# Layer 1 of a two-layer recurrent trunk: one compact tile for an item's beta and kappa, and what the scores and transposes then take

## The chip, the cores and the metric

The kernel runs on one core of a Trainium2 chip. The metric is the device time of one execution in microseconds (us), as a median over runs. The profile is of one execution, and its own time stands beside its span below. Engine names are those of the profile: PE is TensorE's matmul stream and PEld its weight loads, DVE is VectorE, ACT is ScalarE, POOL is GpSimd, SP is the queue that issues most DMAs.

## The reference

Layer 0 is a gated DeltaNet mixer, layer 1 an RWKV-7 mixer, then a final RMSNorm; 1024 prompt tokens behind 16 meta tokens and 8 samples of 8 tokens go through both, 1104 tokens in all. The change lies in layer 1. Cut to what matters, it computes for 16 heads of 64 channels:

```python
kk = l2norm((k * k_k).reshape(B, T, H, N))
k = k * (1.0 + (a - 1.0) * k_a)
decay = jnp.exp(-jnp.exp(w))
b_h = kk * a_h
def step(S, inp):
    S = (S * d_t[:, :, None, :]
         + jnp.einsum('bhvk,bhk->bhv', S, -kk_t)[..., None] * b_t[:, :, None, :]
         + v_t[..., None] * k_t[:, :, None, :])
    return S, jnp.einsum('bhvk,bhk->bhv', S, r_t)
```

and, behind the scan, a norm per head, a bonus term, a gate and the projection `y @ w_o`.

## The kernel before, in words

Everything is float32; large projections are split into a high and a low part of a faster format (fp32r), so a product is three matmuls (`whi`/`wlo` are the parts of a weight, `d`, `dz`, `zz` their outputs). Two stages matter here. Up to about 1885 us of the span run layer 0, the projections of layer 1 and the inverses of the chunks' triangular matrices. From there to the end runs layer 1's recurrence, in `layer1`, and with it the gate projections of the later token segments (`zz`), the output projection (`d<-yh`, `d<-yl`) and the final norm (`dfin`).

The recurrence works on 24 items: 3 token segments (384, 384, 336 tokens) times 8 pairs of heads. An item is a tile of 128 rows, 64 channels of each of the two heads, by 384 tokens, which are 6 chunks of 64. For each item `rwkv_front` prepares:

- `AR`, per chunk 64 columns of decayed alpha and 64 of decayed receptance;
- beta and kappa (`BK`), 64 columns each per chunk: the key times an inverse decay, by DVE, and the rate times the normalised key, by POOL. There are two persistent tiles `BK[0]` and `BK[1]` of 128 rows each. They are zeroed once (L1715), and an item writes rows 0 to 63 of the one and rows 64 to 127 of the other, so that a matmul over 128 rows of `BK[h]` sees head h alone;
- scores `G` = BK' AR, a 128x128 block for each chunk and head: 12 matmuls over 128 rows, three to a PSUM tile, masked into SBUF by DVE;
- `BT`, the transposed BK: 12 transposes, one per chunk and head, of a head's 64 rows;
- `UV`, whose first 64 rows are the transposed v: 6 transposes, one per chunk, into two PSUM tiles.

All these PSUM tiles share the name `f`, of which there are two buffers; so the third tile waits until the first has been copied out. `rwkv_step` then does one chunk of one item (outputs `rA`; `rX`, `UV`, `rS` on the way), and three items are in their steps at any time. `rwkv_finish` ends an item (`zyT`, `yh`, `yl`). A float32 matmul is two instructions on PE (two passes), a transpose one.

The Python loop over `tau` names the work, but the order on each engine is set when the program is built, by a scheduler that goes through the instructions with times of its own. So an edit of the front also moves other instructions. Each engine then runs its own list in order and waits on semaphores. In the listings the numbers behind names tell copies of a tile apart; the scores of the item numbered 10 (the third pair of the second segment) are `G_26195` before and `G_26080` after.

In the profile a matmul's form is written as rows*columns of the stationary operand, then the moving one: `128*64 128x128` has 128 rows, 64 columns, and 128 moving columns. I call rows*columns its tile shape. `64*128` stands for a head's 64 rows.

Of the kernel before, what the change touches and what calls it, by code (L numbers as in the profile page):

```python
# [11 lines left out]
ALU = mybir.AluOpType  # L12
# [23 lines left out]
class Builder:  # L36
# [8 lines left out]
    def t(self, pool, shape, tag, bufs=1, dt=F32):  # L45
        self.uid += 1
        return pool.tile(shape, dt, name=f"{tag}_{self.uid}", tag=tag, bufs=bufs)
# [1275 lines left out]
    def rwkv_front(self, p, s):  # L1323
        nc, t, ap, col = self.nc, self.t, self.ap, self.pcol
        P = Ctx()
        P.n = 8 * s + p
        NB = self.NB
        pc = lambda n: col[n][:, p:p + 1]
        P.TT = t(ap, [128, 6, 64], "rTT", 3)
        nc.sync.dma_start(P.TT.rearrange("p c k -> p (c k)"), self.ttd[P.n])  # L1330
        ld = self.rwkv_load(P.n, ap, "f", ("cs", "k", "a", "r", "v"))
        kk, Dp, iD = self.rwkv_keys(p, ld, ap, "f")
        DC = P.DC = t(ap, [128, 14], "DC", NB + 2)
        nc.gpsimd.tensor_copy(DC[:, 0:6].unsqueeze(2), Dp[:, 1:385].rearrange("p (c k) -> p c k", k=64)[:, :, 63:64])
        if s == 0:
            nc.gpsimd.tensor_copy(DC[:, 6:14].unsqueeze(2), Dp[:, 1:65].rearrange("p (c k) -> p c k", k=8)[:, :, 7:8])
        AR = P.AR = t(ap, [128, 6, 2, 64], "AR", NB)
        c6 = lambda x: x.rearrange("p (c k) -> p c k", k=64)
        self.alpha(AR[:, :, 0, :], kk, Dp, s, nc.gpsimd)
        nc.vector.tensor_tensor(AR[:, :, 1, :], c6(ld["r"]), c6(Dp[:, 1:385]), op=ALU.mult)  # L1340
        k2 = t(ap, [128, 384], "k2", 1)
        self.act(k2, ld["a"], AF.Identity, scale=pc("rwkv_k_a"), bias=self.omka[:, p:p + 1])
        nc.vector.tensor_tensor(k2, k2, ld["k"], op=ALU.mult)
        nc.gpsimd.tensor_tensor(kk, kk, ld["a"], op=ALU.mult)

        for h in (0, 1):
            q = slice(64 * h, 64 * h + 64)
            nc.vector.tensor_tensor(self.BK[h][q, :, 0, :], c6(k2)[q], c6(iD)[q], op=ALU.mult)
            nc.gpsimd.tensor_tensor(self.BK[h][q, :, 1, :], c6(kk)[q], c6(iD)[q], op=ALU.mult)
        flat = lambda x: x.rearrange("p x k -> p (x k)")  # L1350

        pr = t(ap, [128, 384], "pr", 1)
        nc.vector.scalar_tensor_tensor(pr, ld["r"], pc("rwkv_r_k"), k2, op0=ALU.mult, op1=ALU.mult)
        bp = self.ps("f", 2, "bonus")
        ph, pl = t(ap, [128, 384], "prh", 1, F32R), t(ap, [128, 384], "prl", 1, F32R)
        self.split(pr, ph, pl, "act", "pool")
        self.mm(bp[:, 0:384], self.bones, ph, start=True, stop=False)
        self.mm(bp[:, 0:384], self.bones, pl, start=False, stop=True)
        bv = P.bv = t(ap, [128, 384], "rbv", NB + 1)
        nc.vector.tensor_tensor(bv, ld["v"], bp[:, 0:384], op=ALU.mult)  # L1360

        G = P.G = t(ap, [128, 6, 2, 128], "G", NB)
        for c in (0, 3):
            for h in (0, 1):
                gp = self.ps("f", 2, "G")
                for u in range(3):
                    self.mm(gp[:, 128 * u:128 * u + 128], flat(self.BK[h][:, c + u]), flat(AR[:, c + u]))
                g3 = gp[:, 0:384].rearrange("p (q k) -> p q k", k=128)
                f = 0
                if s == 0 and c == 0:  # L1370
                    nc.vector.tensor_tensor(G[:, 0, h, :], g3[:, 0, :], self.gms, op=ALU.mult)
                    f = 1
                nc.vector.tensor_tensor(G[:, c + f:c + 3, h, :], g3[:, f:3], self.gm.unsqueeze(1).broadcast_to([128, 3 - f, 128]),
                                        op=ALU.mult)

        BT = P.BT = t(ap, [128, 6, 128], "BT", NB)
        UV = P.UV = self.UVs[P.n % len(self.UVs)]
        for h in (0, 1):
            q = slice(64 * h, 64 * h + 64)
            tp = self.ps("f", 2, "BT")  # L1380
            for c in range(6):
                self.transpose(tp[:, 64 * c:64 * c + 64], flat(self.BK[h][q, c]))
            nc.scalar.copy(BT[:, :, q], tp[:, 0:384].rearrange("p (c k) -> p c k", k=64))
        for c in (0, 3):
            vp = self.ps("f", 2, "VT")
            for u in range(3):
                self.transpose(vp[0:64, 128 * u:128 * u + 128], ld["v"][:, 64 * (c + u):64 * (c + u) + 64])
            nc.scalar.copy(UV[0:64, c:c + 3].rearrange("p c h k -> p (c h k)"), vp[0:64, 0:384])
        return P

    def rwkv_step(self, p, s, P, ci):
# [289 lines left out]
    def layer1(self, ctx, right, stay, xa, xb, x):  # L1681

        nc, tc = self.nc, self.tc
# [6 lines left out]
        for n, (m, k) in enumerate(todo):  # L1690
            if k == 0:
                x = self.mix(m, xb)
# [14 lines left out]
        t, ap = self.t, self.ap  # L1707
# [2 lines left out]
        self.X = [t(ap, [128, 2, 64], f"rX{q}") for q in range(4)]  # L1710
        NB = self.NB = 4
        self.UVs = [t(ap, [128, 6, 2, 64], f"UV{q}") for q in range(NB)]
        self.BK = [t(ap, [128, 6, 2, 64], f"BK{q}") for q in (0, 1)]
        for x in self.BK + self.X + self.UVs + self.S:
            nc.vector.memset(x, 0.0)  # L1715
        P, yo, todo = {}, {}, []
        gates = (None for s in (1, 2) for _ in self.rwkv_gates(xa, s, self.fin))
# [3 lines left out]
        for tau in range(-LAG * AHEAD, LAG * 24 + 6):  # L1721
            n = tau // LAG + AHEAD
            if tau % LAG == 0 and 0 <= n < 24:
                s, p = divmod(n, 8)
# [10 lines left out]
            for n in range(max(0, (tau - 5 + LAG - 1) // LAG), min(24, tau // LAG + 1)):  # L1735
                s, p = divmod(n, 8)
# [53 lines left out]
```

## Time and profile before

| what | value |
|---|---|
| median of 3 runs | 2517.23 us (2510.52 to 2519.47) |
| the profiled execution: its own time | 2503.36 us |
| its span | 2501.6 us |
| granted TensorE clock over the span | 0.968 |
| PE busy | 2305.2 us (92%), 18593 instructions |
| DVE, ACT, POOL busy | 1698.5 (68%), 1423.3 (57%), 1148.4 us (46%) |

The profile page gives for each engine how long at least one of its instructions was under way. On PE instructions overlap: one that lasts 275 ns may have its successor start 112 ns later. So for the cost of a matmul what counts is the distance from its start to the start of the next. The timeline view lists start and length of each group of like instructions; the start of the row below less the start of a row is what the group took of PE.

### The profile page before, as it was taken

To read this page: it belongs to the slowest core of one execution; us is meant where nothing else is said; L and a number is where in the kernel's file an instruction comes from. 1 tells how busy PE (TensorE), PEld (TensorE's weight loads), DVE (VectorE), ACT (ScalarE), POOL (GpSimd) and SP (SyncE) were. 2 spreads that over 40 slices of the span, in tenths; PEclk is the share of its full clock that TensorE was granted. 3 is DMA by queue.
4 is the path that set the end of the run, shared out by engine and by line. 5 is a ranking of instruction groups with operands and counts; after the bars stand their busy time and mean duration, and the time that the engine had idled before them with its cause. 6 is when DMAs were issued, how large, how long until landed. Compare 5 with 4: busy or idle time off the path is not lost. (4 is left out here: it accounts for less than half of the span.)

```text
span 2501.6 us, 52567 instructions
## 1 busy us (share of the span) xinstructions
PE 2305.2 (92%) x18593; PEld 2065.5 (83%) x18593; DVE 1698.5 (68%) x4268; ACT 1423.3 (57%) x3913; POOL 1148.4 (46%) x1404
## 2 busy tenths in 40 slices
PE   6998999999898989999989999988879999999996
PEld 5887988888797889789989998877768777877875
DVE  7779686876849585863357535697875678667563
ACT  5456555564646565565344557464444567678663
POOL 4554444444444354432214425453347565656653
PEclk9999999999999999999999999999988999999997
DMA  3323333333232333353251445767565444343331
GB/s 107 100 72 98 83 106 83 95 85 85 79 91 77 87 89 85 92 147 118 89 147 60 117 167 180 170 184 202 145 181 170 126 133 121 94 140 88 110 97 50
DMA packets 471939, 284.65 MB, mean 114 GB/s; under 512 B 187482, under 2 KB 457051, under 8 KB 471675
## 3 DMA queue, kind: packets, MB, share of 16 engines
q1 hardware_dynamic: 471674, 281.29, 40.0%
q8 instruction: 147, 2.41, 0.4%
q14 instruction: 118, 0.96, 0.1%
HBM read 200.00 MB, written 81.17 MB: 112 GB/s over the span
## 5 line engine op out<-in xcount | busy, mean ns | idle before, releaser
L86 POOL TENSOR_TENSOR wlo<-wraw,whi 128x512 fp32r<-128x512 f32 x260 | 347.8, 1340 | 350.9 <-ACT whi L82 311.9
L82 ACT CAST whi<-wraw 128x512 fp32r<-128x512 f32 x260 | 160.1, 617 | 168.7 <-PE dq L76 43.6
L76 PE MATMUL d<-xc,whi 128*128 128x384 f32 (+3 forms) x846 | 238.2, 339 | 0.3 <-ACT ev L1152 0.3
L450 DVE TENSOR_TENSOR invtmp<-invA,invT 72x31 f32<-72x31 f32 (+31 forms) x403 | 184.7, 458 | 20.8 <-DMA invA<-ltd 7.6
L452 DVE TENSOR_TENSOR invT<-invT,invtmp 72x31 f32<-72x31 f32 (+31 forms) x403 | 187.6, 466 | 6.9
L76 PEld LDWEIGHTS d<-xc,whi 128*128 128x128 f32 (+1 forms) x846 | 155.0, 190 | 7.3 <-issue 4.6
L76 PE MATMUL dz<-xc,whi 128*128 128x384 f32 (+1 forms) x480 | 149.6, 343 | 0.0
L76 PE MATMUL dv<-xc,whi 128*128 128x384 f32 (+1 forms) x480 | 149.4, 343 | 0.0
L417 DVE SCALAR_TENSOR_TENSOR cvy<-raw,cw,cvy 128x408 f32<-128x408 f32 (+2 forms) x192 | 128.9, 674 | 28.7 <-POOL cvy L415 27.4
L76 PE MATMUL dz<-xa,whi 128*128 128x384 f32 (+1 forms) x416 | 139.4, 357 | 4.8 <-ACT whi L82 2.4
L76 PE MATMUL d<-xa,whi 128*128 128x384 f32 (+3 forms) x450 | 140.0, 344 | 3.9 <-ACT xa L82 2.5
L415 POOL TENSOR_TENSOR cvy<-cvy,cvz 128x408 f32<-128x408 f32 (+2 forms) x96 | 99.7, 1039 | 70.5 <-ACT cvz L62 51.3
L76 PE MATMUL d<-xc,wlo 128*128 128x384 f32 (+2 forms) x396 | 130.5, 339 | 0.0
L76 PE MATMUL rA<-rS,AR 128*64 128x128 f32 x512 | 106.0, 289 | 8.7 <-DVE rS L1439 5.0
L76 PE MATMUL rA<-UV,G 128*64 128x64 f32 x1152 | 112.4, 223 | 0.4 <-ACT UV L62 0.4
L76 PE MATMUL dv<-xa,whi 128*128 128x384 f32 (+1 forms) x288 | 101.4, 352 | 8.9 <-ACT raw L401 6.9
L76 PEld LDWEIGHTS rA<-UV,G 128*64 128x64 f32 x1152 | 101.7, 138 | 3.3 <-issue 1.4
L62 ACT ACTIVATE o<-rA,gcol 128x128 f32<-128x128 f32 x128 | 46.2, 367 | 90.0 <-DVE S L774 89.6
L62 ACT ACTIVATE raw<-cvy 128x408 f32<-128x408 f32 (+2 forms) x96 | 49.5, 516 | 82.1 <-DVE cvy L417 80.6
L1439 DVE SCALAR_TENSOR_TENSOR rS<-rA,DC,pre 64x64 f32<-64x64 f32 x256 | 72.2, 282 | 31.6 <-PE rA L76 26.6
L62 ACT ACTIVATE rX<-rA,rk 64x64 f32<-64x64 f32 x272 | 83.7, 308 | 16.9 <-PE rA L76 10.9
L76 PE MATMUL dz<-xa,wlo 128*128 128x384 f32 (+1 forms) x256 | 90.5, 354 | 2.9 <-POOL wlo L86 2.9
(510 smaller groups left out, 7730.1 us busy)
## 6 DMA issues: line engine op xcount, KB each, us to landing
wraw<-in_gdn_w_in SPq DMA_DIRECT2D x96, 256.0 KB
wraw<-in_rwkv_w_rkvz SPq DMA_DIRECT2D x96, 256.0 KB
Sb<-in_state_gdn SPq DMA_DIRECT2D x64, 256.0 KB
wraw<-in_rwkv_w_o SPq DMA_DIRECT2D x48, 256.0 KB
E<-drow SPq DMA_DIRECT2D x24, 384.0 KB
attn<-drow SPq DMA_DIRECT2D x24, 384.0 KB
wraw<-in_gdn_w_out SPq DMA_DIRECT2D x36, 256.0 KB
out_s_gdn<-Sb SPq DMA_DIRECT2D x32, 256.0 KB
```

Of the source, the lines that this page charges most:

```text
L62: return self.nc.scalar.activation(out, in_, func, bias=bias, scale=scale, **kw)
L76: self.nc.tensor.matmul(out, lhsT, rhs, start=start, stop=stop)
L82: nc.scalar.copy(hi, x)
L86: e.tensor_tensor(lo, x, hi.bitcast(F32), op=ALU.subtract)
L415: nc.gpsimd.tensor_tensor(y[:, 0:wd], y[:, 0:wd], y1[:, 0:wd], op=ALU.add)
L417: nc.vector.scalar_tensor_tensor(y[:, 0:wd], raw[:, k:k + wd], cw[k], y[:, 0:wd], op0=ALU.mult, op1=ALU.add)
L450: nc.vector.tensor_tensor(tmp, A[:, j, j + 1:32].unsqueeze(2).broadcast_to([nb, n, m]), Tv[:, j, 0:m].unsqueeze(1).broadcast_to([nb, n, m] ...
L452: nc.vector.tensor_tensor(Tv[:, j + 1:32, 0:m], Tv[:, j + 1:32, 0:m], tmp, op=ALU.subtract)
L1439: nc.vector.scalar_tensor_tensor(S[hs[h], h, :], dS, DC[hs[h], ci:ci + 1], pre[hs[h], hs[h]], op0=ALU.mult, op1=ALU.add)
```

## The change: what it does

The two zero-padded tiles go. An item's beta and kappa are written as one tile of 128 rows, two buffers in turn, with one DVE and one POOL instruction over 128 rows in place of two over 64 each. A head's scores contract over its 64 rows alone. The transposes of BK take 128 rows and 128 columns at once, 6 for 12, and three chunks share a PSUM tile. The transposes of v take two chunks at once, 3 for 6, in one PSUM tile for two; two copies take the even and the odd chunks out of it. `rwkv_step` stays.

```diff
-        for h in (0, 1):
-            q = slice(64 * h, 64 * h + 64)
-            nc.vector.tensor_tensor(self.BK[h][q, :, 0, :], c6(k2)[q], c6(iD)[q], op=ALU.mult)
-            nc.gpsimd.tensor_tensor(self.BK[h][q, :, 1, :], c6(kk)[q], c6(iD)[q], op=ALU.mult)
+        BK = t(ap, [128, 6, 2, 64], "BK", 2)
+        nc.vector.tensor_tensor(BK[:, :, 0, :], c6(k2), c6(iD), op=ALU.mult)
+        nc.gpsimd.tensor_tensor(BK[:, :, 1, :], c6(kk), c6(iD), op=ALU.mult)
...
         for c in (0, 3):
             for h in (0, 1):
                 gp = self.ps("f", 2, "G")
+                q = slice(64 * h, 64 * h + 64)
                 for u in range(3):
-                    self.mm(gp[:, 128 * u:128 * u + 128], flat(self.BK[h][:, c + u]), flat(AR[:, c + u]))
+                    self.mm(gp[:, 128 * u:128 * u + 128], flat(BK[q, c + u]), flat(AR[q, c + u]))
...
-        for h in (0, 1):
-            q = slice(64 * h, 64 * h + 64)
+        for c in (0, 3):
             tp = self.ps("f", 2, "BT")
-            for c in range(6):
-                self.transpose(tp[:, 64 * c:64 * c + 64], flat(self.BK[h][q, c]))
-            nc.scalar.copy(BT[:, :, q], tp[:, 0:384].rearrange("p (c k) -> p c k", k=64))
-        for c in (0, 3):
-            vp = self.ps("f", 2, "VT")
             for u in range(3):
-                self.transpose(vp[0:64, 128 * u:128 * u + 128], ld["v"][:, 64 * (c + u):64 * (c + u) + 64])
-            nc.scalar.copy(UV[0:64, c:c + 3].rearrange("p c h k -> p (c h k)"), vp[0:64, 0:384])
+                self.transpose(tp[:, 128 * u:128 * u + 128], flat(BK[:, c + u]))
+            nc.scalar.copy(BT[:, c:c + 3], tp[:, 0:384].rearrange("p (c k) -> p c k", k=128))
+        vp = self.ps("f", 2, "VT")
+        for u in range(3):
+            self.transpose(vp[:, 128 * u:128 * u + 128], ld["v"][:, 128 * u:128 * u + 128])
+        for a in (0, 1):
+            nc.scalar.copy(UV[0:64, a:6:2].rearrange("p c h k -> p c (h k)"),
+                           vp[64 * a:64 * a + 64, 0:384].rearrange("p (c k) -> p c k", k=128))
...
-        self.BK = [t(ap, [128, 6, 2, 64], f"BK{q}") for q in (0, 1)]
-        for x in self.BK + self.X + self.UVs + self.S:
+        for x in self.X + self.UVs + self.S:
             nc.vector.memset(x, 0.0)
```

The order of the instructions moves too. On PE, where the scores and transposes of item 10 stand among the steps of the items ahead of it (`rA`), the list before reads, from its first scores on:

```order
L76 MATMUL fG_26196<-AR_26172,BK_4216_22905 128x128 x3
L76 MATMUL rA_26261<-rX_4208_22897,rTT_25661 64x128
L76 MATMUL rA_26280<-rX_4209_22898,rTT_25913 64x128
L76 MATMUL rA_26243<-rS_4207_22896,AR_25389 64x128
L76 MATMUL rA_26243<-UV_4215_22904,G_25413 64x64 x2
L76 MATMUL rA_26243<-UV_4215_22904,BT_25436 64x64 x2
L76 MATMUL fG_26201<-AR_26172,BK_4217_22906 128x128 x3
L76 MATMUL rA_26261<-rS_4200_22889,AR_25682 64x128
```

The same place on PE after the change, item 10 again:

```order
L76 MATMUL fG_26081<-AR_26058,BK_26066 128x128 x3
L76 MATMUL fG_26086<-AR_26058,BK_26066 128x128 x3
L76 MATMUL rA_26118<-rS_4207_22896,AR_25308 64x128
L76 MATMUL rA_26118<-UV_4215_22904,G_25331 64x64 x2
L76 MATMUL rA_26118<-UV_4215_22904,BT_25354 64x64 x2
L76 MATMUL rA_26155<-rX_4209_22898,rTT_25810 64x128
L73 MATMUL zyT_25988<-ident_74,y_25445 128x128 x3
L76 MATMUL rA_26136<-rS_4200_22889,AR_25590 64x128
```

The blocks of the first head (`fG_26196`, then `fG_26081`) and the second (`fG_26201`, then `fG_26086`) had a step's work between them and now follow each other directly.

Further down the same list on PE, before, stand item 10's transposes:

```order
L73 MATMUL fBT_26217<-ident_74,BK_4216_22905 128x64 x6
L76 MATMUL rA_26371<-rS_4201_22890,AR_25934 64x128
L76 MATMUL rA_26371<-UV_4213_22902,G_25957 64x64 x2
L73 MATMUL fBT_26225<-ident_74,BK_4217_22906 128x64 x6
L76 MATMUL rA_26298<-rS_4207_22896,AR_25389 64x128
L76 MATMUL rA_26298<-UV_4215_22904,G_25413 64x64 x2
L76 MATMUL rA_26298<-UV_4215_22904,BT_25436 64x64 x2
L76 MATMUL rA_26353<-rX_4208_22897,rTT_25661 64x128
L73 MATMUL fVT_26233<-ident_74,fldv_26161 64x128 x3
L73 MATMUL zyT_26102<-ident_74,y_25537 128x128 x3
L76 MATMUL rA_26371<-rX_4209_22898,rTT_25913 64x128
L73 MATMUL fVT_26238<-ident_74,fldv_26161 64x128 x3
```

And after:

```order
L73 MATMUL fBT_26102<-ident_74,BK_26066 128x128 x3
L76 MATMUL rA_26173<-rX_4211_22900,rTT_25286 64x128
L76 MATMUL rA_26246<-rS_4201_22890,AR_25831 64x128
L76 MATMUL rA_26246<-UV_4213_22902,G_25853 64x64 x2
L73 MATMUL fBT_26107<-ident_74,BK_26066 128x128 x3
L76 MATMUL rA_26228<-rX_4208_22897,rTT_25569 64x128
L73 MATMUL fVT_26112<-ident_74,fldv_26047 128x128 x3
```

Two blocks of six small transposes and two of three for v became two blocks of three large ones and one of three for v.

On DVE, the next item's beta stood behind the last scores of item 10 before:

```order
L1373 TENSOR_TENSOR G_26195<-fG_26206,gm_22861 128x3x128
L1439 SCALAR_TENSOR_TENSOR rS_4201_22890<-rA_26280,DC_25932,pre_26286 64x64 x2
L102 SCALAR_TENSOR_TENSOR grs_26095<-gn_t_26097,grs_26095 128x6
L1373 TENSOR_TENSOR G_26195<-fG_26211,gm_22861 128x3x128
L1348 TENSOR_TENSOR BK_4216_22905<-k_4949_26454,fiD_26444 64x6x64
L1348 TENSOR_TENSOR BK_4217_22906<-k_4949_26454,fiD_26444 64x6x64
L1340 TENSOR_TENSOR AR_26450<-fldr_26437,fDp_26443 128x6x64
```

After, on DVE:

```order
L1373 TENSOR_TENSOR G_26080<-fG_26086,gm_22861 128x3x128
L1439 SCALAR_TENSOR_TENSOR rS_4207_22896<-rA_26118,DC_25305,pre_26124 64x64 x2
L1347 TENSOR_TENSOR BK_26333<-k_4947_26329,fiD_26319 128x6x64
L1466 SCALAR_TENSOR_TENSOR t_4871_25994<-zyT_25988,lnw_22883,rbv_25046 128x384
L1439 SCALAR_TENSOR_TENSOR rS_4200_22889<-rA_26136,DC_25588,pre_26142 64x64 x2
L1373 TENSOR_TENSOR G_26080<-fG_26091,gm_22861 128x3x128
```

It is one instruction now, in the middle of item 10's scores, since it no longer writes a tile that item 10's transposes still have to read.

Over the whole recurrence, counted in PE's list: before, the 96 blocks of scores stand in 12 pairs (6 matmuls in a row for two heads) and 72 alone; after, in 31 pairs (two of them short by one matmul) and 34 alone, and 2 single matmuls. Neighbours of different tile shape meet 477 times before and 465 times after. A block of scores or pair is entered from another tile shape 57 times and left for another 67 times before, 67 and 67 after; a block of BK's transposes 48 and 48 before, 28 and 22 after.

## The prediction

> **What bounds the kernel now.** I read the page's busy times first, then the busy times in the stretch in which the changed code runs, then the waits there, and last PE's timeline around single fronts. The page's first line for the whole span, and the stretch of the recurrence up to its last front beside what comes after (columns: length, busy time and instructions of each engine, granted clock, DMA):
>
> ```profile
> PE 2305.2 (92%) x18593; PEld 2065.5 (83%) x18593; DVE 1698.5 (68%) x4268; ACT 1423.3 (57%) x3913; POOL 1148.4 (46%) x1404
> ...
> 1885.00:2415.00 530.00, 504.42 (x4499) 425.26 (x4500) 370.60 (x1024) 353.87 (x978) 318.57 (x356) 0.99 0.41 120
> 2415.00:2501.60 86.60, 63.29 (x468) 53.78 (x466) 34.11 (x126) 34.90 (x104) 34.40 (x33) 0.85 0.20 60
> ```
>
> In these 530 us PE is busy for 504.4, 95%, at a clock of 0.99; DVE has 70%, ACT 67%, POOL 60%. So the stage is bound by PE, and an instruction taken from PE is worth nearly its distance to the next. What PE still waits for there, the longest line and the one on the tile ring, and the longest waits of DVE and POOL that touch the change:
>
> ```profile
> PE rA L76 <- ACT rX L62: 6.2, 16, 1.2
> ...
> PE fG L76 <- DVE G L1373: 1.9, 2, 1.3
> ...
> PE fG L76 <- POOL BK L1349: 0.5, 1, 0.5
> ...
> DVE BK L1348 <- PE fBT L73: 20.7, 18, 3.2
> ```
>
> PE waits little for anything. DVE stands 20.7 us because the padded tile is still read by PE's transposes; PE did not stand still in that time, so this wait going is not a gain by itself.
>
> **The price of a block on PE.** Start to start, from the timeline (start, length, form, count). Scores between neighbours of the same shape, and scores and transposes between other shapes:
>
> ```profile
> 2215.66 0.83 PE L76 MATMUL fG<-AR,BK 128*128 128x128 f32 x6
> 2216.33 0.60 PE L73 MATMUL dfin<-ident,x 128*128 128x128 f32 x4
> ...
> 2163.37 0.94 PE L76 MATMUL fG<-AR,BK 128*128 128x128 f32 x6
> 2164.24 0.58 PE L73 MATMUL fBT<-ident,BK 64*128 64x64 f32 x6
> 2164.75 0.44 PE L76 MATMUL d<-yh,wlo 128*128 128x384 f32 x1
> ```
>
> Six passes of scores take 2216.33 - 2215.66 = 0.67 us, 0.11 a pass, where the shape stays, and 2164.24 - 2163.37 = 0.87 where it is entered from another shape and left for another: 0.10 for each side. Six small transposes take 0.51. The Trainium skill says as much of the sides: TensorEngine Tiling (Array Packing), Key Properties, has it that a change of tiling mode drains the array, and this trace agrees with 0.10 a side. That rule speaks against the change, which takes the scores out of the shape that the projections have; by it alone, with nothing overlapped, the scores would cost 1.4 us more (below). Now large transposes, and those of v:
>
> ```profile
> 2087.59 0.58 PE L73 MATMUL fBT<-ident,BK 64*128 64x64 f32 x6
> 2088.11 0.55 PE L73 MATMUL zyT<-ident,y 128*128 128x128 f32 x3
> 2088.49 0.49 PE L73 MATMUL fVT<-ident,fldv 128*64 128x128 f32 x3
> 2088.91 0.43 PE L76 MATMUL rA<-rX,rTT 128*64 128x128 f32 x2
> ...
> 2215.34 0.49 PE L73 MATMUL dfin<-ident,x 128*128 128x128 f32 x3
> ...
> 2279.77 0.52 PE L73 MATMUL fVT<-ident,fldv 128*64 128x128 f32 x3
> 2280.12 0.49 PE L73 MATMUL zyT<-ident,y 128*128 128x128 f32 x3
> 2280.54 0.32 PE L76 MATMUL rA<-rX,rTT 128*64 128x128 f32 x1
> ```
>
> Three transposes of 128x128, as the new ones will be, take 0.32 (`dfin`, shape kept) to 0.38 and 0.42 (`zyT`); three of v now 0.42 and 0.35.
>
> The last price is the one that matters most: two blocks of 64 rows, one on rows 0 to 63 and one on rows 64 to 127, directly behind each other. Before, that happens once in full, with the transposes; beside it twelve passes of scores over 128 rows:
>
> ```profile
> 1921.22 0.77 PE L73 MATMUL fBT<-ident,BK 64*128 64x64 f32 x12
> 1921.91 0.45 PE L76 MATMUL zz<-xa,whi 128*128 128x384 f32 x1
> ...
> 1893.54 1.50 PE L76 MATMUL fG<-AR,BK 128*128 128x128 f32 x12
> 1894.97 0.99 PE L76 MATMUL drsr<-AR,Sb 64*64 64x16 f32 x26
> ```
>
> Twelve small transposes of the two heads took 0.69, not 2 x 0.52: the second head's ran beside the first's and cost 0.17 more than one block alone. Twelve passes over 128 rows took 1.43, all in a row.
>
> **The change, part by part.**
>
> *Scores.* Passes and columns stay; I take 0.11 a pass over 64 rows too, as the small transposes are streamed no slower per column. Before: 96 blocks x 0.67 + (57 + 67) sides x 0.10 = 76.7 us. After: 34 lone blocks x 0.87 = 29.6; two single matmuls 2 x (0.22 + 0.20) = 0.8; 31 pairs. If the two heads run beside each other as in the row of 1921 us, a pair is 0.87 + 0.17 = 1.04, together 32.2. Sum 62.6: 14.1 us less. If nothing overlaps, a pair is 1.34 + 0.20 = 1.54, the sum 78.1: 1.4 more. I take the overlap, because the row has just this shape and just this pairing.
>
> *Transposes of BK.* Before 46 blocks x 0.52 + 0.69 = 24.6. After 48 blocks between 0.32 and 0.42; as about half their sides are switches, 0.38: 18.2, so 6.4 less (4 to 9).
>
> *Transposes of v.* Before 48 blocks x 0.39 = 18.7, after 24 x 0.38 = 9.1: 9.6 less (7 to 11).
>
> *The neighbours' sides.* 477 switches have 954 sides, of which the scores and transposes of BK and v hold 262 before (57 + 67, 48 + 48, and 20 + 22 for v's, counted in the same lists); of 930 sides after they hold 67 + 67, 28 + 22 and 12 + 16 = 212. So others get 718 - 692 = 26 sides x 0.10 = 2.6 us more.
>
> PE's work: -14.1 - 6.4 - 9.6 + 2.6 = **-27.5 us**; without overlap -12.0.
>
> *DVE and POOL.* The rows of the two writes, and one instruction over 128 rows on each engine as the price of the new ones (busy, mean ns); and the zeroing:
>
> ```profile
> L1348 DVE TENSOR_TENSOR BK<-k,fiD 64x384 f32<-64x384 f32 x48 | 33.6, 699 | 21.1 <-PE fBT L73 20.7
> L1340 DVE TENSOR_TENSOR AR<-fldr,fDp 128x384 f32<-128x384 f32 x24 | 22.6, 943 | 22.6 <-PE rA L76 14.4 <-ACT fDp L62 4.2 <-DMA fldr<-rd 3.7
> ...
> L1349 POOL TENSOR_TENSOR BK<-fkk,fiD 64x384 f32<-64x384 f32 x48 | 49.7, 1036 | 4.1 <-PE fBT L73 2.1
> L1271 POOL TENSOR_TENSOR AR<-fkk,fDp 128x384 f32<-128x384 f32 x24 | 29.2, 1218 | 38.9 <-PE rA L76 37.9 <-ACT fkk L62 0.7
> ...
> 1864.26 1.50 DVE L1715 MEMSET BK<- 128x768 f32 x2
> ```
>
> DVE 33.6 to 22.6, POOL 49.7 to 29.2, 1.5 of zeroing gone. All costed at nothing, since PE's 95% covers it; were that cover gone, DVE's 20.7 us of waiting and these 11 would be the most they could give. I leave up to 8 of it in the low end. The first scores now wait for both heads' halves together; behind them stands PE's whole list, but the halves come 2 x 1.036 - 1.218 = 0.85 us earlier on POOL, and that wait was 0.5 us in all.
>
> *ACT* makes the same four copies of 384 columns an item, of PSUM tiles of which there are eight in place of nine. Loads and stores stay.
>
> *From work to time.* I take four fifths of the 27.5: PE's idle 25.6 us of 530 and its waits on `rX` show that the steps' own chains sometimes set the pace, and they do so oftener when the fronts fill less. 22 us. The profiled execution took 2503.4 us, 13.9 under the median of 2517.2; its 22 us are subtracted from the median: **2495 us**. Three fifths give 2501, all of it and the 8 us give 2482.
>
> **The rivals.**
>
> *The second head starts behind the first.* If the second block starts only with the first one's last pass, a pair is 0.87 + 5 x 0.11 = 1.42 and the scores come to 74.4, 2.3 less; the sum is -15.7, of which four fifths are 12.6: 2505 us, on the edge of what can be told from no change. For it: it's one row against it, and with smaller matmuls. Against: in that row the saving is 0.34 us of 1.03, too much for one pass. The Trainium skill's TensorE: Matmul & The Clock Gate, Part 3, "What overlaps and what doesn't", would give this rival: matmuls start and end strictly in program order there. The row of 1921 us does not agree.
>
> *PE's time turns into waiting.* The steps' chain from PE over `rX` and `UV` on ACT to `rS` on DVE sets the pace, and a fifth of the work comes out as time: 5 us, 2512. For it: the waits on `rX`, the longest of PE's. Against: 6.2 us of 530.
>
> *The tile ring stops PE: slower.* Paired scores fill both `f` tiles in 1.04 us, and the third block must wait until DVE has masked the first. Before, this happened so:
>
> ```profile
> 2156.89 0.94 PE L76 MATMUL fG<-AR,BK 128*128 128x128 f32 x6
> 2159.14 0.94 PE L76 MATMUL fG<-AR,BK 128*128 128x128 f32 x6 [1.31 <-DVE G L1373]
> ```
>
> Two such stops an item, at the second pair and at the first transposes, are 48 x 1.31 = 62.9 us, less 22: 2558. It decides from (22 + 12.6) / 1.31 = 26 stops, about one an item. Against: the list of item 10 has eight rows of other work between the second block and the third (six of them are shown above), and the waits show 1.9 us in two stops.
>
> **How the numbers follow.** Forecast 0.60, the second head behind the first 0.17, waiting 0.15, the ring 0.08. A measurement of this kernel tells about 0.5% (12.6 us) from no change: the forecast is faster, the second case half and half, the third the same, the fourth slower: 0.68, 0.24, 0.08. The likeliest case gives 2482 to 2501; the second's 2505 and the third's 2512 are taken in, the ring's left out: 2482 to 2512.
>
> **What would show it.** Groups `fG` with 64*128 whose pairs take about 1.04 us start to start (1.42 or 1.54 if the rivals hold); `fBT` and `fVT` at 128*128 with 144 and 72 instructions, 0.32 to 0.42 for three; PE's busy time from 1885 us to the last front shorter by some 20 us with its share still about 95%; no line "DVE BK <- PE fBT". I am wrong if the pairs do not overlap, if PE's share falls to 92% at the same length, or if "PE fG <- DVE G" grows to tens of us.

## The result, and the profile after

| what | before | after |
|---|---|---|
| median, 7 runs each in turn on one chip | 2514.37 us (2505.54 to 2519.47) | 2497.78 us (2490.95 to 2507.27) |
| ratio of after to before, 95% interval | | 0.9941 [0.9918, 0.9964] |
| the profiled execution: its own time, span | 2503.36, 2501.6 us | 2496.27, 2494.6 us |
| first `zz` to the end of the span | 636.0 us | 623.8 us |

The change is faster by 0.6% (14.8 us by the ratio; a second set of runs of the same kernel, below, gave 0.7%). The prediction was 2495 us, with 2482 to 2512 as its range. The two spans differ by 7.0 us only, since a profile is of one execution: that of before lies 11.0 us under its median, that of after 1.5 us under its own, and of the kernels below that of `one_buffer` is the quickest of its 12 and those of `bk_alone`, `same_head` and `transposes_twice` are the slowest of theirs. The first `zz`, which the change does not touch, came 5.0 us earlier in before; over all kernels below it came between 1863.6 and 1880.0 us, behind 13569 instructions on PE in each. So stage lengths here count from the first `zz`.

The page's first line of after, and the recurrence in the same stretch as in the prediction:

```profile
PE 2288.1 (92%) x18377; PEld 2048.2 (82%) x18377; DVE 1666.5 (67%) x4242; ACT 1423.5 (57%) x3913; POOL 1116.7 (45%) x1380
...
1885.00:2415.00 530.00, 498.09 (x4348) 416.28 (x4350) 339.62 (x1004) 359.46 (x986) 295.95 (x344) 0.98 0.42 122
```

PE is busy 17.1 us less over the span, and in the stretch its share fell from 95% to 94%. From 1885 us to the last front it is busy for 491.1 us of 523, where before has 504.4 of 530: 13.3 us less, and the forecast had some 20. The groups that the change touches, first of before, then of after (busy time, mean of one, idle time of the engine ahead of them):

```profile
L76 PE MATMUL fG<-AR,BK 128*128 128x128 f32 x576 | 85.7, 288 | 2.8 <-DVE G L1373 1.9 <-POOL BK L1349 0.5 <-DVE rX L1415 0.3
L73 PE MATMUL fBT<-ident,BK 64*128 64x64 f32 x288 | 28.1, 233 | 0.0
L73 PE MATMUL fVT<-ident,fldv 128*64 128x128 f32 x144 | 24.9, 285 | 0.9 <-ACT BT L1383 0.7
```

```profile
L76 PE MATMUL fG<-AR,BK 64*128 64x128 f32 x576 | 72.2, 291 | 4.1 <-DVE G L1373 3.8 <-POOL BK L1348 0.2
L73 PE MATMUL fBT<-ident,BK 128*128 128x128 f32 x144 | 24.6, 283 | 1.2 <-DVE G L1373 1.2
L73 PE MATMUL fVT<-ident,fldv 128*128 128x128 f32 x72 | 12.5, 283 | 0.2
L1347 DVE TENSOR_TENSOR BK<-k,fiD 128x384 f32<-128x384 f32 x24 | 17.9, 747 | 6.5 <-PE fBT L73 3.3 <-ACT fiD L62 2.8
L1348 POOL TENSOR_TENSOR BK<-fkk,fiD 128x384 f32<-128x384 f32 x24 | 25.0, 1040 | 0.4 <-PE fBT L73 0.2
```

One instruction over 128 rows costs DVE 747 ns, against 699 for each of the two over 64 rows before; POOL 1040 against 1036. Start to start and summed over the stage (each instruction's distance to the next one on PE), scores went from 81.1 to 68.2 us, transposes of BK from 24.8 to 19.4, those of v from 21.0 to 9.5. I call these three the blocks: 126.9 to 97.1 us, 29.8 less.

Half of that is missing in the time. Part of it shows at the steps (`rA`). The groups that wait, first of before, then of after:

```profile
L76 PE MATMUL rA<-rS,AR 128*64 128x128 f32 x512 | 106.0, 289 | 8.7 <-DVE rS L1439 5.0 <-ACT UV L62 1.7 <-ACT y L1441 1.5
L76 PE MATMUL rA<-rX,rTT 128*64 128x128 f32 x288 | 55.9, 291 | 8.2 <-ACT rX L62 8.2
```

```profile
L76 PE MATMUL rA<-rS,AR 128*64 128x128 f32 x512 | 106.9, 291 | 16.6 <-ACT UV L62 8.3 <-DVE rS L1439 6.3 <-ACT y L1441 0.6
L76 PE MATMUL rA<-rX,rTT 128*64 128x128 f32 x288 | 55.0, 290 | 6.2 <-ACT rX L62 6.1
```

The steps' matmuls take no longer, but PE stands idle 22.8 us ahead of these two groups, for 16.9 before. What grew is the wait for `UV` (1.7 to 8.3 us); that for `rX` fell from 8.2 to 6.1. Start to start the steps take 239.0 us for 223.8, 15.2 more. With a usual distance of each form taken off, some 8 to 9 us of that are longer waits, some 3 more switches of tile shape at their sides, and some 3 matmuls that no longer overlap; the split moves by as much as 1 us with what is taken as usual.

Single blocks, from the timeline of after:

```profile
2137.88 1.26 PE L76 MATMUL fG<-AR,BK 64*128 64x128 f32 x12
2139.07 0.43 PE L76 MATMUL rA<-rX,rTT 128*64 128x128 f32 x2
...
2140.56 0.93 PE L76 MATMUL fG<-AR,BK 64*128 64x128 f32 x6
2141.43 0.43 PE L76 MATMUL rA<-rS,AR 128*64 128x128 f32 x2
```

A lone block takes 0.87 us, as foreseen; a pair 1.19, between the 1.04 of the forecast and the 1.42 of its first rival (1.19 is also the median of all 29 full pairs). By the starts of the twelve instructions in the trace, the distances in the pair are 213, 112, 6, 105, 108, 4, 108, 4, 107, 112, 112 and 201 ns. They come apart into two rows of six with the same distances, 213, 112, 111, 112, 112 ns, the second 331 ns behind the first; and the ninth and the twelfth to start, the last of each row, are the two that signal a finished PSUM tile. So the second head's first pass starts 6 ns behind the first head's third.

### The profile page after: what moved, and what is told of

The parts are those of the page before. It is cut to its first block, busy times and chain, and to the rows that moved or that the text cites. A ratio compares the mean times of both kernels' runs of the same rounds, so it can differ in the third digit from the quotient of the medians.

```text
span 2494.6 us, 52030 instructions
## 1 busy us (share of the span) xinstructions
PE 2288.1 (92%) x18377; PEld 2048.2 (82%) x18377; DVE 1666.5 (67%) x4242; ACT 1423.5 (57%) x3913; POOL 1116.7 (45%) x1380
## 5 line engine op out<-in xcount | busy, mean ns | idle before, releaser
L76 PE MATMUL rA<-rS,AR 128*64 128x128 f32 x512 | 106.9, 291 | 16.6 <-ACT UV L62 8.3
L76 PEld LDWEIGHTS dz<-xc,whi 128*128 128x128 f32 x480 | 92.0, 197 | 0.7
```

The costliest lines, as they stand in the source:

```text
L76: self.nc.tensor.matmul(out, lhsT, rhs, start=start, stop=stop)
```

## The experiments

Two questions: do the heads' passes really run beside each other, and where is the other half of the blocks' time? For the second there were three theories: the steps' chain takes up about half of what PE is spared; the 64-row scores cost TensorE's clock; or another order of the same instructions moves the time as much as the change. The letters A, B, C in the last four expectations name these three, in this order; theories 1 and 2 of the earlier ones are said in that of `v_alone`. "At half clock" is time in which the trace's clock record shows 0.5. "The stage's middle" is from 25 to 575 us behind the first `zz`: in after 13.6 us of it are at half clock, in before 6.8.

All in one table. Blocks are start to start in the profiled execution; the clock is the granted clock's mean over the span and all runs. The kernels were run in several sets, each beside runs of before, whose median was 2510.7 to 2514.4 us by set. A ratio is taken within a set; the first line of the table has the median of all 88 runs of before in the later sets.

| kernel | median us | ratio to before, 95% | blocks us | clock |
|---|---|---|---|---|
| before | 2511.7 | | 126.9 | 0.9673 |
| after | 2497.8 | 0.9941 [0.9918, 0.9964] | 97.1 | 0.9671 |
| after_again | 2496.9 | 0.9931 [0.9913, 0.9949] | 96.7 | 0.9678 |
| v_alone | 2502.0 | 0.9960 [0.9938, 0.9981] | 111.8 | 0.9685 |
| bk_alone | 2514.5 | 1.0006 [0.9992, 1.0021] | 116.4 | 0.9637 |
| same_head | 2513.0 | 1.0001 [0.9985, 1.0018] | 113.9 | 0.9646 |
| alt_bdvd | 2501.9 | 0.9953 [0.9938, 0.9968] | 89.5 | 0.9630 |
| transposes_twice | 2516.2 | 1.0008 [0.9988, 1.0028] | 129.9 | 0.9682 |
| one_buffer | 2509.1 | 0.9982 [0.9962, 1.0002] | 99.4 | 0.9649 |
| null_order | 2500.0 | 0.9952 [0.9935, 0.9969] | 121.8 | 0.9678 |
| heads_swapped | 2508.8 | 0.9987 [0.9968, 1.0005] | 123.3 | 0.9669 |
| after_null | 2507.3 | 0.9978 [0.9962, 0.9995] | 100.7 | 0.9637 |
| alt_null | 2505.3 | 0.9982 [0.9962, 1.0001] | 94.3 | 0.9657 |
| scores_128 | 2518.9 | 1.0029 [1.0015, 1.0043] | 111.9 | 0.9667 |

Since one profile is not always typical, times are compared by medians and ratios; the profiles serve for prices and waits.

### The same kernel again

> The changed kernel once more, on the chip and beside the runs of the kernels of this group, so that they can be compared with it directly. All theories: 0.994 of the kernel before, within 0.002, and again 68 us of PE for the scores, 19 and 10 for the transposes of BK and v.

0.9931 beside 0.9941: the two sets agree, and the gain is 0.6 to 0.7%, 15 to 17 us.

### The parts alone

`v_alone` is the kernel before with v's transposes of the change; `bk_alone` is the change with v's transposes as before:

```diff
 v_alone, against before
 ...
-            for u in range(3):
-                self.transpose(vp[0:64, 128 * u:128 * u + 128], ld["v"][:, 64 * (c + u):64 * (c + u) + 64])
 ...
+        for u in range(3):
+            self.transpose(vp[:, 128 * u:128 * u + 128], ld["v"][:, 128 * u:128 * u + 128])
 ...
```

> The kernel before with the transposes of v alone changed (3 of 128x128 for 6; padded tiles, scores and BK's transposes as before). Theory 1, the gain comes from PE's work in the front's blocks: of the 29.8 us that those blocks lost start to start, v's transposes have 11.5; v's 72 transposes should take 9 to 11 us in this run, and at the rate seen so far (14.8 us of time for 29.8 of work) the time should fall by 6 us against the kernel before (3 to 11). Theory 2, the gain comes from the tile being free sooner and from DVE's and POOL's halved writes: no change, and DVE's wait for BK's transposes stays near 20 us.

> The changed kernel with v's transposes as before (six of a chunk, two PSUM tiles): beta and kappa compact, scores over 64 rows, BK's transposes large. 29 pairs in PE's list. Theory 1 (PE's blocks): v's take 21 us again, so 11 us of PE's saving is missing, 19 us stay; time 5 to 10 us under the kernel before, 4 to 9 over the changed one. If the two parts help each other only together (no gain here, though the blocks are 19 us shorter), the steps' chains or the order took it back, and PE's busy or waiting time of the steps' matmuls must be up by as much.

The smallest part alone gave two thirds of the gain: 0.9960, with blocks 15.1 us shorter. The larger part gave nothing: 1.0006, with blocks 10.5 us shorter. So v's transposes came out as theory 1 had them (10 us for 3 to 11), the rest did not (none for 5 to 10). The two do not add up in any simple way, and `bk_alone` has one of the lowest clocks of the table. In its profile the steps take 239.7 us start to start for 223.8 before, and there is a long stretch at half clock in the middle of the stage (columns: window, its length, busy PE, PEld, DVE, ACT, POOL, granted clock, DMA):

```profile
2057.50:2061.00 3.50, 2.87 (x32) 2.27 (x30) 3.43 (x8) 0.79 (x2) 3.35 (x6) 1.00 0.80 228
2061.00:2064.40 3.40, 2.16 (x28) 1.59 (x28) 1.56 (x11) 3.25 (x8) 3.11 (x6) 1.00 0.97 310
2064.40:2084.90 20.50, 18.66 (x109) 15.02 (x109) 10.07 (x31) 8.68 (x25) 4.86 (x5) 0.50 0.23 60
2084.90:2105.00 20.10, 19.56 (x211) 14.68 (x207) 16.33 (x51) 14.26 (x40) 9.23 (x13) 1.00 0.36 103
```

PE stood still for 36% of the 3.4 us ahead of it, and the next 20.5 us ran at half clock: 109 instructions in them, 211 in the 20.1 us behind.

### Do the two heads run beside each other?

`same_head` puts the loop over heads outside, so that two blocks in a row are one head's, on the same rows. `alt_bdvd` lets the passes alternate between the heads (and moves the bonus and v's tiles to another PSUM name, so that two score tiles can be open at once):

```diff
 same_head, against after
-        for c in (0, 3):
-            for h in (0, 1):
+        for h in (0, 1):
+            for c in (0, 3):
 alt_bdvd, against after
+            gps = [self.ps("f", 2, "G") for _ in (0, 1)]
+            for u in range(3):
+                for h in (0, 1):
+                    q = slice(64 * h, 64 * h + 64)
+                    self.mm(gps[h][:, 128 * u:128 * u + 128], flat(BK[q, c + u]), flat(AR[q, c + u]))
 ...
```

> The changed kernel with the two blocks of one head issued behind each other, then the other head's: as many pairs in PE's list (31), but both halves of a pair on the same 64 rows, so that they cannot run beside each other. If the overlap of the two heads is what makes a pair 1.19 us, pairs here take 1.43 to 1.54 us start to start, PE's scores 8 to 11 us more than in the changed kernel, and the time 4 to 11 us more than that kernel's. If pairs are short for another reason, both stay.

> The changed kernel with the two heads' score matmuls alternating in the source (u outside, h inside, both PSUM tiles at once) and the bonus and v's transposes on the two PSUM buffers of tag d in place of f, so that only scores and BK's transposes share f. PE's list has 34 pairs, and neighbours of another tile shape 427 times against 465. If pairs that alternate run beside each other from the first pass, a pair takes 0.95 to 1.0 us in place of 1.19; with 3 more pairs the scores come to about 60 us (68 in the changed kernel), and 76 fewer sides are another 7 us: 15 us of PE. At half of it in time, 7 us faster than the changed kernel (2 to 14); were the rings of d in the way of the output projection, slower than it.

Twelve passes, first of `same_head`, then of `alt_bdvd`:

```profile
1942.76 1.60 PE L76 MATMUL fG<-AR,BK 64*128 64x128 f32 x12
1944.29 1.11 PE L76 MATMUL drsr<-AR,Sb 64*64 64x16 f32 x32
```

```profile
1914.80 0.94 PE L76 MATMUL fG<-AR,BK 64*128 64x128 f32 x12
1915.67 0.66 PE L73 MATMUL dsn<-ident,sn 128*128 128x128 f32 x4
```

On the same rows twelve passes take 1.53 us, the serial price; alternating between the halves they take 0.87, that of six. These are also the medians of all such blocks, 30 and 33. So the overlap is shown, and the written order decides how much of it is had: 1.19 where one head's six stand ahead of the other's. The times do not follow as neatly. With `same_head` scores took 83.3 us and the gain was gone: the time is 15 to 18 us over after's by the ratios, where 30 pairs x 0.34 us are 10 and 4 to 11 were expected, so more than the overlap went. With `alt_bdvd` scores took 60.0, 8 us less than in after, but the time, for which 7 us less were expected, was no better than after's. Its steps wait longer, 33.6 us ahead of the two groups for 22.8 in after:

```profile
L76 PE MATMUL rA<-rS,AR 128*64 128x128 f32 x512 | 107.7, 294 | 15.9 <-ACT UV L62 6.2 <-ACT y L1443 5.1 <-DVE rS L1441 3.3
L76 PE MATMUL rA<-rX,rTT 128*64 128x128 f32 x288 | 58.5, 295 | 17.7 <-ACT rX L62 15.7 <-DVE rX L1417 1.5
```

### More work, and one buffer

```diff
 transposes_twice, against after (transposes of BK and of v; each result written a second time)
-            for u in range(3):
+            for u in (0, 1, 2, 0, 1, 2):
 one_buffer, against after
-        BK = t(ap, [128, 6, 2, 64], "BK", 2)
+        BK = t(ap, [128, 6, 2, 64], "BK", 1)
```

> The changed kernel with each transpose of BK and v issued twice into the same place: 216 more transposes of 0.11 us, 24 us of PE, and as fewer scores stand in pairs then (23 for 31) some 28 to 33 us in all. If the stage is bound by PE, the time rises by 24 to 33 us over the changed kernel. If PE's work comes out as time by half, as the change's did, by 12 to 17. If the steps' chains set the pace, by under 8.

> The changed kernel with one buffer for BK in place of two: the next item's beta must wait again until this item's transposes have read the tile. Theory 2 (free sooner) expects the gain to go, wholly or by half: 7 to 15 us slower than the changed kernel, and DVE's wait for BK's transposes back at 15 to 20 us. Theory 1 expects within 5 us of the changed kernel. A third view, that the second buffer lets DVE's list put the next item's beta ahead of this item's masks and so stops PE at the start of the stage (3.1 us there), expects it 2 to 5 us faster.

Twice the transposes: blocks are 32.8 us longer than in after (129.9 for 97.1), and the time is 17 to 19 us longer by the ratios, 0.5 to 0.6 us of time for one of PE. With one buffer the time is 10 to 13 us over after's by the ratios, so that the gain over before can no longer be told from none. That is the time that theory 2 gave, but not its cause: DVE's wait for BK's transposes is 7.4 us, for 3.3 in after and 20.7 before, and not 15 to 20. The third view had it faster; the stop at the start of the stage is indeed gone (the longest wait of scores for a mask is 0.8 us), and the time rose all the same. Whether the buffer does that or the order that comes with it is not settled: its blocks are nearly as short as after's, and its steps wait 27.0 us for 22.8.

### Another order of the same instructions

`null_order` is the kernel before with v's transposes written ahead of BK's, `after_null` is the same edit of after, and `heads_swapped` is the kernel before with head 1 written ahead of head 0 in scores and transposes. No instruction is added or removed; the scheduler makes other lists of them.

```diff
 null_order, against before (after_null likewise: the two groups of transposes change places)
+        for c in (0, 3):
+            vp = self.ps("f", 2, "VT")
 ...
         for h in (0, 1):
             q = slice(64 * h, 64 * h + 64)
             tp = self.ps("f", 2, "BT")
 ...
-        for c in (0, 3):
-            vp = self.ps("f", 2, "VT")
 heads_swapped, against before
-            for h in (0, 1):
+            for h in (1, 0):
```

> The kernel before with v's transposes written ahead of BK's in the source: the same instructions, in another order throughout, since the scheduler places them anew. Neighbours of another tile shape stand 496 times in PE's list against 473 when counted the same way, 4.6 us of sides. This measures what an order alone can do: if the theories that count PE's work hold, 2 to 5 us slower than the kernel before; if the scheduler's luck is as large as the gain, it may move by 10 us either way with no change in the blocks' prices.

> The kernel before with head 1 written ahead of head 0 in scores and transposes: the same instructions, another order by the scheduler (27 pairs of scores stand directly behind each other on PE for 12). Theory A: no change, 0.998 to 1.002. Theory B: no change, no more than 7 us at half clock between 25 and 575 us of the stage. Theory C: 0.3 to 0.5% from the kernel before in either direction; with fewer switches of tile shape in the list (461 against 473, 24 sides of 0.10 us) rather below, 0.995 to 0.998.

> The changed kernel with the transposes of v written ahead of those of BK: the same instructions, another order by the scheduler. Theory A: as the changed kernel, ratio 0.992 to 0.996. Theory B: as the half-clock stretches fall: 13.6 us of them in the changed kernel; each 10 us more or less move the time by about 5 us, 0.2%. Theory C: it differs from the changed kernel by 0.3 to 0.5% in either direction, 0.989 or 0.999, with the same PE time for scores and transposes (68, 19, 9.5 us).

`null_order` is 0.48% faster than before, nearly as much as the change, where the theories that count PE's work had it 2 to 5 us slower. Its profile shows the same groups at nearly the same price:

```profile
L76 PE MATMUL fG<-AR,BK 128*128 128x128 f32 x576 | 85.2, 288 | 0.2
L73 PE MATMUL fBT<-ident,BK 64*128 64x64 f32 x288 | 27.5, 231 | 0.1
L73 PE MATMUL fVT<-ident,fldv 128*64 128x128 f32 x144 | 23.9, 277 | 0.0
L76 PE MATMUL rA<-rS,AR 128*64 128x128 f32 x512 | 106.1, 289 | 10.9 <-DVE rS L1439 5.3 <-ACT UV L62 2.5 <-ACT y L1441 1.2
L76 PE MATMUL rA<-rX,rTT 128*64 128x128 f32 x288 | 56.1, 290 | 5.3 <-ACT rX L62 5.1
```

Here some waits went: 2.8 to 0.2 us ahead of the scores, 8.2 to 5.3 ahead of `rA<-rX`, while those ahead of `rA<-rS` rose from 8.7 to 10.9. Blocks are 5.1 us shorter, and there is no stretch at half clock in the stage's middle. DVE's wait for BK's transposes is all there (22.6 us for 20.7), so 12 us can come without theory 2's relief. `heads_swapped` moved by 0.13%, not told from no change. `after_null` loses more than half of the gain (0.9978), with 100.7 us of blocks for 97.1, a wait on `rX` of 10.9 us where after has 6.2, and a lower clock:

```profile
L76 PE MATMUL fG<-AR,BK 64*128 64x128 f32 x576 | 72.2, 294 | 4.0 <-DVE G L1373 3.8
L76 PE MATMUL rA<-rX,rTT 128*64 128x128 f32 x288 | 57.8, 297 | 10.9 <-ACT rX L62 10.8
```

That is what theory C gave, 0.3 to 0.5% from the changed kernel. So order alone is worth up to half a per cent in either kernel. Averaged over the orders tried, the kernel before stands at 0.9980 (1, 0.9952, 0.9987) and the changed one at 0.9957 (0.9936 of two sets, and 0.9978): 0.2%, some 6 us, is what five orders leave to the change itself, with a spread as large as that.

### Scores as before with the new transposes; and alternating passes in another order

`scores_128` keeps the padded tiles for the scores and writes the compact tile besides, for the transposes. `alt_null` is after with alternating passes (as `alt_bdvd`, PSUM names as in after) and v's transposes ahead of BK's.

```diff
 scores_128, against after
+        for h in (0, 1):
+            q = slice(64 * h, 64 * h + 64)
+            nc.vector.tensor_tensor(self.BK[h][q, :, 0, :], c6(k2)[q], c6(iD)[q], op=ALU.mult)
+            nc.gpsimd.tensor_tensor(self.BK[h][q, :, 1, :], c6(kk)[q], c6(iD)[q], op=ALU.mult)
 ...
-        pr = t(ap, [128, 384], "pr", 1)
+        pr = k2
 ...
-                    self.mm(gp[:, 128 * u:128 * u + 128], flat(BK[q, c + u]), flat(AR[q, c + u]))
+                    self.mm(gp[:, 128 * u:128 * u + 128], flat(self.BK[h][:, c + u]), flat(AR[:, c + u]))
 ...
```

> The change's transposes with the scores as before: the compact tile is written for the transposes, the two padded tiles are written as before for the scores (two more DVE and two more POOL instructions an item; to make room, the compact tile has one buffer, the bonus product is written over the keys and its result has four buffers for five). Scores over 128 rows, about 81 us start to start; transposes of BK 19 to 21 and of v 9 to 10, so 16 to 17 us less of PE than before. Theory A (PE's work is worth about half, because the steps' chain takes up the rest): 8 us less, ratio 0.996 to 0.998. Theory B (64-row scores with pauses let the clock gate halve the clock for stretches, and that eats what they save): no or hardly any stretches at half clock between 25 and 575 us of the stage (0 to 7 us against 13.6), and a ratio no worse than the whole change's 0.994. Theory C (the scheduler's order alone moves the time by half a per cent): anywhere from 0.991 to 1.001.

> The changed kernel with the two heads' passes alternating (pass u of head 0, then of head 1) and the transposes of v ahead of those of BK: 434 switches of tile shape against 465, so 62 sides x 0.10 = 6 us less beside scores of about 60 us for 68. Blocks and sides together some 44 us of PE below the kernel before. Theory A: half of it, 22 us, ratio 0.991. Theory B: 64-row scores leave 13 to 40 us at half clock, of which half is lost beyond what the kernel before loses: 0.993 to 0.998. Theory C: 0.986 to 0.996 around A's value. If it comes under 0.992 it beats both kernels.

`scores_128` is slower than before by 0.3%, which none of the three theories gave, though its blocks are 15.0 us shorter. Its steps wait more:

```profile
L76 PE MATMUL rA<-rS,AR 128*64 128x128 f32 x512 | 108.5, 295 | 19.3 <-DVE rS L1443 8.7 <-ACT y L1445 4.3 <-ACT UV L62 3.9
L76 PE MATMUL rA<-rX,rTT 128*64 128x128 f32 x288 | 58.7, 298 | 11.4 <-ACT rX L62 9.1 <-DVE rX L1419 2.0
```

30.7 us ahead of the two groups, for 16.9 before. The kernel gives DVE and POOL an added two instructions an item and has one buffer less here and there, so its loss cannot be put down to one of these or to its order. It speaks against theory B: scores over 128 rows, and 30.7 us at half clock in the stage's middle. Nor do 64-row scores always bring much more than before's 6.8: `alt_null`, with 64-row scores throughout, has 10.2, less than the 11.1 of `heads_swapped` with 128-row ones. So 64-row scores are not what such stretches need. That they bring some is not ruled out: the nine kernels of the table with 64-row scores have a mean clock of 0.9654, the other five 0.9674, which is some 10 us more at half clock.

`alt_null` has blocks 32.6 us shorter than before and fewer switches of tile shape than after (434 for 465), and gains 0.18%, its interval reaching 1; only the upper edge of theory B's range comes near that. PE waits 31.4 us ahead of its steps' two groups. It and `alt_bdvd` have the shortest blocks of the table, and neither is faster than after.

### What the table says together

Fitted over the 14 medians of the table, one us less of blocks gives 0.29 us of time, and that explains only 29% of the variance. The clock alone explains 5%, the two together more: taking 2 x (1 - clock) x time as a kernel's time at half clock, the fit gives 0.42 us for each us of blocks and 0.42 for each us at half clock, and 56% of the variance, with `scores_128` 11.5 us above it and `null_order` 8.7 below. Between runs of one kernel, over 222 executions, the time follows the clock too: 0.30 us for each us at half clock, correlation 0.72. So 0.3 to 0.4 of the blocks' time came through on average (with a standard error of 0.13), and what is left over is nearly as large as the gain.

Where the rest goes shows in the waits at the steps. Over the 14 profiles, PE's idle time ahead of the two groups `rA<-rS` and `rA<-rX` rises by 0.33 us for each us by which the blocks are shorter (correlation -0.77): 15.8 to 16.9 us in before, `null_order` and `heads_swapped`, 22.8 in after, 31.4 and 33.6 in `alt_null` and `alt_bdvd`, whose blocks are the shortest. That is theory A's mechanism, with `scores_128` (30.7 us) well off the line. These are fits, with blocks and waits from one execution each; they show what goes together, not what causes it.

## Why the prediction was right, and where it was not

- **PE bounds the stage, and blocks get shorter.** Right, and well sized: -27.5 us with the neighbours' sides, against -29.8 for the blocks and some 2 us more of others' sides (26 of them by the lists; the 2 us are an estimate).
- **Scores, -14.1.** -12.9. The lone blocks' 0.87 held. The pair was undersized: 1.19 us for 1.04, because the model row (twelve small transposes, 0.17 for the second six) was carried over to passes that start beside each other only from the third on. 31 pairs x 0.15 us are 4.6 us. That the sum still came close is luck: before's scores took 81.1 us where the forecast's prices give 76.7, so 4.4 us of waits and the like, and after's 68.2 where its prices with the measured pair give 67.2, so 1.0. That these 3.4 us would go was not foreseen.
- **Sides of 0.10.** Held: 213 ns for the first pass into `64*128`, where 112 is a pass. The Trainium skill's TensorEngine Tiling (Array Packing), Key Properties, has that drain; the measured price is this.
- **Transposes of BK -6.4, of v -9.6.** -5.4 and -11.5. Before's v took 21.0 us and not 18.7: two of its 48 blocks had 0.9 and 1.0 us of idle time behind them, and after has no such wait.
- **DVE and POOL at nothing.** Busy times fell as said and further (17.9 and 25.0 us for 22.6 and 29.2). "No line DVE BK <- PE fBT" was wrong in the letter: 3.3 us of 20.7 are left, for the two buffers come round too. That the relief is worth nothing by itself is not shown, but the gain does not go with it: `bk_alone` and `same_head` have nearly all of it (3.4 and 3.7 us left) and gain nothing, `null_order` has none (22.6) and gains 12 us.
- **From work to time, four fifths.** This is the step that failed. 14.8 to 17 us came out of 27.5, a little over half, and 17 to 19 of 32.8 us in `transposes_twice`; over the other kernels the share ran from none (`bk_alone`, `same_head`) to two thirds (`v_alone`), so that no fixed share holds. The steps grew by 15.2 us in the same time, a little over half of it waits. The sum was then taken from 2517.2, the median of 3 runs; that of 7 was 2514.4. So the base was 2.8 us high and the gain between the medians (16.6 us for 22) 5.4 short of the forecast; the two errors are of opposite sign for the time, and 2495 stands 2.8 from 2497.8. So close a hit is luck, the more so as an order alone moved `null_order` by 12 us.
- **The rival "PE's time turns into waiting"** had the mechanism that the waits bear out, and the share lies between: neither one fifth came out nor four, but a little over half. It was given 0.15 and should have been weighed more. It pointed at the chain over `rX` and `UV`; in after the wait that grew was on `UV`, and the wait on `rX`, which it gave as its evidence, fell by 2 us.
- **The rival "the second head starts behind the first"** fell: 1.19 us, not 1.42. The Trainium skill's rule in TensorE: Matmul & The Clock Gate, Part 3, that matmuls start in program order, does not hold in this trace: a second block's first pass starts ahead of the first block's fourth, by the two rows of starts above.
- **The ring as a stop** is there once, at the stage's start, and not 26 times:

```profile
1898.22 0.38 PE L73 MATMUL dsn<-ident,sn 128*128 128x128 f32 x2
1901.65 1.62 PE L76 MATMUL fG<-AR,BK 64*128 64x128 f32 x6 [3.05 <-DVE G L1373]
1903.20 0.69 PE L76 MATMUL zz<-xa,whi 128*128 128x384 f32 x1
```

  DVE's new list has work of the next items ahead of the first masks. The next item's beta was done by 1896.53 us, before the first two blocks were; what held the masks up were the rows for `AR` and the keys, which waited for ACT:

```profile
1898.12 1.03 DVE L1340 TENSOR_TENSOR AR<-fldr,fDp 128x384 f32<-128x384 f32 x1 [1.06 <-ACT fDp L62]
1900.15 0.82 DVE L1343 TENSOR_TENSOR k<-k,fldk 128x384 f32<-128x384 f32 x1 [1.00 <-ACT k L62]
1900.90 0.28 DVE L1371 TENSOR_TENSOR G<-fG,gms 128x128 f32<-128x128 f32 x1
```

  So the third block of the first item stood 3.05 us, and from its end on, from 1901.3 to 1908.1 us, the clock record shows 0.5. The line "PE fG <- DVE G" went from 1.9 to 3.8 us over the whole kernel, not to tens.
- **A rival that was missing.** The order that the scheduler makes of any edit. `null_order` shows that a prediction of 0.9% for this kernel should have carried about half a per cent to either side for that alone.

## What to carry to other kernels

Two matmul blocks on different halves of the rows run beside each other, and passes written in turns do so fully (0.87 us for twelve, against 1.19 in two blocks and 1.53 on one half). In a kernel whose order a scheduler makes, an edit's gain of half a per cent cannot be told from a new order; run one or two edits that change the order alone before believing it, and average over orders. Of the work taken from an engine that is 95% busy, do not count on most of it where chains of steps through other engines stand close behind: here a little over half came out in after, 0.3 to 0.4 by the fit over all kernels, and the shorter the blocks were, the longer the steps waited.

## What the runs showed of the hardware that was not expected

The second block does not wait for the first to end, nor does it start at once: its first pass came 6 ns behind the third pass of the first block, and the two then alternate 4 to 6 ns and 105 to 108 ns apart.

TensorE's clock falls to half in the middle of a busy stage. The trace's clock record shows it in multiples of 3.41 us (3.4 to 20.5). In the stage's middle, over the profiles of all kernels together, of 2120 such windows at full clock in which PE was busy for 65% or more, 8 were followed by one at half clock; of 25 with 60 to 65%, 7; of 31 with 50 to 60%, 15; of 15 with less, 13. So idle time of 1.4 us or more within one window (PE busy for under 60%) was followed by a window at half clock in 28 of 46 cases; half a window, 1.7 us, is an estimate of what that costs besides, about as much as the wait. The Trainium skill's TensorE: Matmul & The Clock Gate, Part 1, has a window of about 3.4 us, and the trace agrees with 3.41. Its table has the clock fall after at least one idle window, and here windows in which PE was busy for half the time were often enough.

What stays open: which property of an order makes the steps wait more, how much of the gain is the change's own and how much its order's, and why a stretch at half clock lasts one window in one place and six in another, with PE busy in it.
